# A 31-tap depthwise convolution divided anew between TensorE, VectorE, ScalarE and GpSimd

## The chip, the cores and the metric

The kernel runs on one core of a Trainium2 chip. The metric is the device time of one execution in microseconds, and what is told of a kernel is the median of several runs. All data is float32; a product of a weight matrix with activations is computed as three products of rounded halves ("hi" and "lo" parts), which a later section explains.

## What is computed

The reference is a stack of two transformer-like blocks, each with two layers, over 256 positions and 1024 channels. The change touches only the convolution branch of the second block's mixer. Cut to that:

```python
def depthwise_conv(c, w, b):                      # 31 taps, 512 channels
    pad = CONV_WIDTH_2 // 2                       # 15
    y = lax.conv_general_dilated(c, w.reshape(31, 1, 512), window_strides=(1,),
                                 padding=[(pad, pad)], feature_group_count=512, ...)
    return y + b

def second_block(x, ...):
    for i in range(2):
        h = x + 0.5 * swiglu(rms_norm_2(x, norm_ffn1[i]), w_ffn1_in[i], w_ffn1_out[i])
        u = rms_norm_2(h, norm_mix[i])
        q, k, v, c, g = jnp.split(u @ w_in[i], splits, axis=-1)
        y_attn = window_attention(q, k, v, sink[i], rel_bias) @ w_attn_out[i]
        c_val, c_gate = jnp.split(c, 2, axis=-1)
        c = c_val * jax.nn.sigmoid(c_gate)
        c = depthwise_conv(c, conv_w[i], conv_b[i])
        c = jax.nn.silu(layer_norm_2(c, conv_ln_g[i], conv_ln_b[i]))
        y_conv = c @ w_conv_out[i]
        g_attn, g_conv = jnp.split(jax.nn.sigmoid(g), 2, axis=-1)
        h = h + (g_attn * y_attn + g_conv * y_conv) @ w_o[i]
        ...
```

## The kernel before

Activations lie with channels on the 128 partitions and the 256 positions along the free axis (S = 256), so a convolution along positions is a sum over shifted columns, and one weight per partition. The 512 channels of the convolution are four chunks of 128, c0 to c3 (`conv(i, t)`, i = 0 to 3).

A weight matrix comes in pieces of 128 x 1024 (`wload`, L133). SP issues the transfer into `raw`; ScalarE casts it to `hi` (L145); VectorE makes `lo` = `raw` - `hi` (L146). Six buffers hold such splits, so a cast must wait until TensorE has done the products that read the buffer's old content. `mm3` (L182) then makes three products for each 128 rows: hi with h, hi with l, lo with h (L184, L185, L186), where h and l are the activations' halves (L221, a cast on ScalarE, and L222, a subtraction on VectorE).

`mix_b` is the mixer of the second block. It walks through 15 pairs of output columns of `w_in_2`, 48 products each: q, k and v (pairs 0 to 2), the four chunks of the convolution (3 to 6), and eight pairs of gates (`dp` 0 to 7). Beside them run generators: attention heads (`heads`, `attention_b`), and `conv` for each chunk. The class `Order` (L310) interleaves them: each `yield` names a cost, that cost times a pace of 1.5 sets when the generator is due again, and after each pair the planner moves on by 5.2 and lets all that is due write its instructions. A scheduler then sets the final order within each engine; every engine runs its own queue in order, and semaphores join them.

In `conv`, a chunk's gate is a tanh (L1203), and its product with the values goes into the padded tile `cp`, 286 columns, of which there are three buffers (L1208). The first PTAPS = 7 taps are matmuls: ScalarE makes a diagonal matrix `dg` from the identity and one column of weights (L1214, four buffers), and TensorE multiplies `cp`, shifted by the tap, with it and adds up in a PSUM tile `rec` (L1215). The pool of `rec` has two buffers. ScalarE then copies the sum with the bias into the SBUF tile `cy` (L1218), and VectorE adds the other 24 taps there one behind the other (L1220, `stt`: tap times weight plus `cy`).

When all chunks and heads have written their work, `norm` computes the layer norm over the 512 channels on TensorE: four matmuls with ones for the mean (L1243), four for the variance from squares (L1250, L1251), a square root on ScalarE with a table load of its own (L1254), the reciprocal on VectorE (L1256), then a tanh for silu (L1260) and the split into h and l (L221, L222). Its instructions are placed among the products of `w_mix` with the attention's result (four outputs, 24 products each); the products of `w_mix` with the convolution's result need the split. Elsewhere in the listing, L1104 are transposes of the softmax, L158 the attention's products (through `run`), L1085 to L1098 the softmax, L1107 the copies `pt` of the transposes, and L1233 the tanh of a gate.

Of the kernel before, what the change touches and what calls it, by code (L numbers as in the profile page):

```python
# [8 lines left out]
F32 = mybir.dt.float32  # L9
F32R = mybir.dt.float32r  # L10
AF = mybir.ActivationFunctionType
# [4 lines left out]
MUL, ADD, SUB, MAX = ALU.mult, ALU.add, ALU.subtract, ALU.max  # L16

S = 256
# [4 lines left out]
C1 = -0.5 * math.exp(-0.5)  # L23
ADA_EVERY = 0.67
ADA_BUFS = 2
PTAPS = 7
ADA_PE = 2
FILL = {("f", 0): ((0, 0), (0, 1)), ("f", 1): ((1, 0), (1, 1))}
PBANKS = (4, 2, 2)
# [1088 lines left out]
def mix_b(G, L, x, l, mp, bias, dbg=None):  # L1118
    nc = G.nc
    mm = nc.tensor.matmul  # L1120
    tt = nc.vector.tensor_tensor
    stt = nc.vector.scalar_tensor_tensor
    act = nc.scalar.activation
    ident = G.c("ident", 128)
# [5 lines left out]
    cwh = L.pool.tile([128, 124], F32, tag="cwh", name=G.nm("cwh"))  # L1130
# [68 lines left out]
    cy = [None] * 4  # L1199
    pmu = []  # L1200

    def conv(i, t):
        act(t[:, S:], t[:, S:], AF.Tanh, scale=0.5)  # L1203
        cp = mp.tile([128, S + 30], F32, tag="cp", name=G.nm("cp"), bufs=3)
        nc.vector.memset(cp[:, 0:15], 0.0)
        nc.vector.memset(cp[:, S + 15:], 0.0)
        yield 0.5
        stt(cp[:, 15:S + 15], t[:, S:], 1.0, t[:, :S], ADD, MUL)  # L1208
        dg = []
        yield 1.0  # L1210
        ps = G.rec()
        for jj in range(PTAPS):
            d = mp.tile([128, 128], F32, tag="dg", name=G.nm("dg"), bufs=4)
            act(d, ident, AF.Copy, scale=cwh[:, jj * 4 + i:jj * 4 + i + 1])  # L1214
            mm(ps[:, :S], d, cp[:, jj:jj + S], start=jj == 0, stop=jj == PTAPS - 1)  # L1215
        yield 0.5 * PTAPS
        y = mp.tile([128, S], F32, tag="cy", name=G.nm("cy"), bufs=4)
        act(y, ps[:, :S], AF.Identity, bias=L.col("cb", i))  # L1218
        for jj in range(PTAPS, 31):
            stt(y, cp[:, jj:jj + S], cwh[:, jj * 4 + i:jj * 4 + i + 1], y, MUL, ADD)  # L1220
            yield 0.6
        cy[i] = y

    for i in range(4):
        t = mp.tile([128, 512], F32, tag="cvg", name=G.nm("t"), bufs=1)
        tt(v3(t, 2), v3(pair(3 + i), 2), rb, MUL)
        O.add(f"c{i}", conv(i, t), 0.6)
        O.advance(cost)
# [55 lines left out]
    for dp in range(4):  # L1284
        w = G.wload(G.ins["w_o"][l, dp], 2048)
        for i in range(2):
            ps = G.ps()
# [320 lines left out]
```

## Time and profile before

| | us |
|---|---|
| median of 3 runs | 2260.83 |
| lowest and highest | 2255.63, 2268.85 |
| the profiled execution | 2264.67 |
| its span in the trace | 2262.9 |
| TensorE busy in it | 2204.6 (97%) |
| VectorE busy in it | 1681.6 (74%) |
| ScalarE busy in it | 1276.6 (56%) |

The profile page has for each engine the busy time, its share of the span and the number of instructions. PE is TensorE's matmul side, PEld its weight load, which runs beside it; DVE is VectorE, ACT ScalarE, POOL GpSimd. The two mixers lie at about 1290 to 1470 us and 1870 to 2050 us of the span; the convolution and the norm of the first at 1334 to 1439 us. A row of the timeline has the start, the time of the entry or group, the engine, the line, the operation and its operands; a bracket at the end tells how long the engine was idle before and what released it. Ends of matmuls are modelled, so a group's price is best read from starts. The clock granted to TensorE is nine tenths of full speed or more in every slice of the page, 0.991 over the span.

### The profile page before, as it was taken

Reading aid. Unit: us, or ns where it says so; the run is one execution under the profiler, and the core shown is the slowest. Engines: PE = TensorE matmul, PEld = TensorE weight load, DVE = VectorE, ACT = ScalarE, POOL = GpSimd, SP = SyncE. Lnnn points to the kernel's source line nnn. Section 1 sums busy time; section 2 is a strip of 40 time slices with the busy share of each in tenths; the row PEclk is TensorE's granted clock in tenths of the full one; section 3 lists DMA queues with packets and bytes.
Section 4 is the critical chain, followed back from the end, with each engine's and each line's share of the span. In section 5 each row is a group of like instructions: output and inputs, shape, how many; then the busy total and the mean of one; then the engine's idle time right before and its main releaser. Section 6 shows DMA issues by size and latency. Waiting matters only on the chain.

```text
span 2262.9 us, 46464 instructions
## 1 busy us (share of the span) xinstructions
PE 2204.6 (97%) x18878; PEld 2134.0 (94%) x18878; DVE 1681.6 (74%) x3041; ACT 1276.6 (56%) x2160; POOL 12.7 (1%) x26
## 2 busy tenths in 40 slices
PE   4999999999999999999999999999999999999999
PEld 4989999999888899999999999999999999999999
DVE  5787878877678878876576569976577656997665
ACT  3575645654567645655454567654465446765444
POOL 0000000000000000000100000000000000000000
PEclk9999999999999999999999999999999999999999
DMA  7644457867554356755775652655566565256553
GB/s 281 195 146 145 139 192 263 271 220 260 187 167 145 121 168 227 264 185 157 177 231 159 199 170 88 203 182 177 164 199 196 165 189 177 94 179 198 182 162 120
DMA packets 127522, 415.35 MB, mean 184 GB/s; under 512 B 15019, under 2 KB 17707, under 8 KB 127308
## 3 DMA queue, kind: packets, MB, share of 16 engines
q1 hardware_dynamic: 124668, 407.23, 57.2%
q0 software_dynamic: 768, 2.10, 0.6%
q8 instruction: 148, 2.42, 0.4%
q10 hardware_dynamic: 1872, 3.06, 0.4%
q14 instruction: 66, 0.54, 0.1%
HBM read 408.92 MB, written 3.41 MB: 182 GB/s over the span
## 4 chain that ended last, share of the span: by engine, by line
PE 61%; DVE 2%; ACT 1%; DMA 1%; issue 0%; SPq 0%; ACTq 0%; DVEq 0%
PE ps L184 19%; PE ps L185 19%; PE ps L186 19%; PE aux L158 1%; PE rec L1215 1%; DMA raw<-in_ffn_in 1%; DVE lo L146 1%; ACT hi L145 0%; PE aux L1104 0%; DMA raw<-in_w_out 0%; PE aux L268 0%; DMA raw<-in_ffn_up 0%; DVE cy L1220 0%; ACT dg L1214 0%; PE aux L282 0%
## 5 line engine op out<-in xcount | busy, mean ns | idle before, releaser
L184 PE MATMUL ps<-h,hi 128*128 128x256 f32 x5088 | 1439.1, 284 | 13.7 <-ACT h L221 8.8
L186 PE MATMUL ps<-h,lo 128*128 128x256 f32 x5088 | 1434.0, 282 | 1.2 <-DVE lo L146 1.2
L185 PE MATMUL ps<-l,hi 128*128 128x256 f32 x4032 | 1136.8, 283 | 4.1 <-DVE l L222 3.9
L145 ACT CAST hi<-raw 128x1024 fp32r<-128x1024 f32 (+1 forms) x724 | 704.4, 976 | 629.2 <-PE ps L185 406.4
L146 DVE TENSOR_TENSOR lo<-raw,hi 128x1024 fp32r<-128x1024 f32 (+1 forms) x724 | 819.5, 1134 | 318.8 <-ACT hi L145 316.5
L184 PEld LDWEIGHTS ps<-h,hi 128*128 128x128 f32 x5088 | 961.5, 189 | 25.2 <-ACT h L221 10.2
L186 PEld LDWEIGHTS ps<-h,lo 128*128 128x128 f32 x5088 | 962.0, 189 | 5.3 <-issue 2.2
L185 PEld LDWEIGHTS ps<-l,hi 128*128 128x128 f32 x4032 | 763.4, 189 | 10.2 <-DVE l L222 4.8
L185 PE MATMUL ps<-h,hi 128*128 128x256 f32 x1056 | 298.9, 283 | 0.0
L185 PEld LDWEIGHTS ps<-h,hi 128*128 128x128 f32 x1056 | 198.6, 188 | 1.9 <-issue 0.5
L221 ACT CAST h<-t 128x256 fp32r<-128x256 f32 x148 | 59.6, 405 | 135.4 <-DVE t L1034 93.6
L222 DVE TENSOR_TENSOR l<-t,h 128x256 fp32r<-128x256 f32 x148 | 62.6, 424 | 50.1 <-ACT h L221 50.0
L362 DVE SCALAR_TENSOR_TENSOR ada<-ada,cact 128x1024 f32<-128x1024 f32 x80 | 96.6, 1215 | 2.1 <-DMA ada<-in_w_ada 2.1
L1031 DVE TENSOR_TENSOR t<-ps,r 128x512 f32<-128x512 f32 x88 | 60.7, 690 | 39.3 <-PE ps L186 39.0
L1220 DVE SCALAR_TENSOR_TENSOR cy<-cp,cwh,cy 128x256 f32<-128x256 f32 x192 | 85.1, 477 | 3.2 <-ACT cy L1218 2.9
L235 ACT ACTIVATE t<-x 128x256 f32<-128x256 f32 x96 | 37.6, 406 | 16.8 <-DVE x L1002 7.7
L1034 DVE TENSOR_TENSOR t<-t,t 128x256 f32<-128x256 f32 x88 | 36.8, 419 | 7.2 <-ACT t L1033 7.2
L1033 ACT ACTIVATE t<-t 128x256 f32<-128x256 f32 x88 | 36.2, 412 | 8.5 <-DVE t L1031 7.6
L210 PE MATMUL ps<-hi,h 128*128 128x256 f32 x128 | 37.7, 294 | 0.0
L242 DVE TENSOR_TENSOR t<-t,t 128x256 f32<-128x256 f32 x87 | 36.5, 419 | 1.6 <-ACT t L237 0.3
L212 PE MATMUL ps<-lo,h 128*128 128x256 f32 x128 | 37.4, 293 | 0.0
L248 PE MATMUL aux<-ones,t 128*128 128x1 f32 x68 | 11.0, 267 | 20.9 <-DVE t L242 17.5
(325 smaller groups left out, 1959.8 us busy)
## 6 DMA issues: line engine op xcount, KB each, us to landing
raw<-in_w_in SPq DMA_DIRECT2D x176, 512.0 KB, 4.4
raw<-in_ffn_in SPq DMA_DIRECT2D x176, 512.0 KB, 4.5
raw<-in_ffn_up SPq DMA_DIRECT2D x88, 512.0 KB, 4.6
ada<-in_w_ada SPq DMA_DIRECT2D x80, 512.0 KB, 5.0
raw<-in_ffn_out SPq DMA_DIRECT2D x64, 384.0 KB, 3.1
raw<-in_ffn_out SPq DMA_DIRECT2D x64, 320.0 KB, 3.1
raw<-in_w_branch SPq DMA_DIRECT2D x24, 512.0 KB, 3.8
raw<-in_ffn_down SPq DMA_DIRECT2D x32, 384.0 KB, 3.5
```

What stands on the lines that cost most here:

```text
L145: nc.scalar.copy(hi[:, :m], raw[:, :m])
L146: nc.vector.tensor_tensor(lo[:, :m], raw[:, :m], hi[:, :m], SUB)
L184: mm(ps, w[0], x[0], start=first, stop=False)
L185: mm(ps, w[0], x[1], start=False, stop=False)
L186: mm(ps, w[1], x[0], start=False, stop=last)
L210: mm(ps[:, :256], x[k][0][:, sl], h, start=k == 0, stop=False)
L221: nc.scalar.copy(h, src)
L222: nc.vector.tensor_tensor(l, src, h, SUB)
L235: nc.scalar.square(sq, x[k])
L362: nc.vector.scalar_tensor_tensor(raw, raw, 1.0, cact, MUL, MUL, accum_out=mods[f // 8][:, f % 8:f % 8 + 1]))
L1031: nc.vector.tensor_tensor(v3(gu, 2), v3(ps, 2), rb, MUL)
L1220: stt(y, cp[:, jj:jj + S], cwh[:, jj * 4 + i:jj * 4 + i + 1], y, MUL, ADD)
```

## The change

Two constants replace PTAPS = 7: PTAPS = 5 and GTAPS = 8. For each chunk, five taps are diagonals and matmuls into `acc`, the first 256 columns of a `rec` tile. The next 18 taps are VectorE's; each reads and writes `acc` in that same PSUM bank. The last eight taps (jj = 23 to 30) are ScalarE's: the first writes tap times weight plus bias straight into `y`, the tile `cy`; the other seven write into a tile `cyt`, of which there is one buffer, and GpSimd adds that to `y`. In the end VectorE adds `acc` and `y` into `y`. Since `rec` has two buffers, chunks 2 and 3 wait in the plan until the chunk two before them is done. Line numbers move: the diagonals are L1226 in the new code, their matmuls L1227, VectorE's taps L1233, the closing addition L1235, the first scaled tap L1214, the others L1217, GpSimd's additions L1218, the gate's tanh L1247, the mean L1257, the squares L1264, the variance L1265, the square root L1268 and the norm's tanh L1274.

```diff
-PTAPS = 7
+PTAPS, GTAPS = 5, 8
...
         stt(cp[:, 15:S + 15], t[:, S:], 1.0, t[:, :S], ADD, MUL)
-        dg = []
+        def wt(jj):
+            return cwh[:, jj * 4 + i:jj * 4 + i + 1]
+
+        def other(jj):
+            if jj == 31 - GTAPS:
+                act(y, cp[:, jj:jj + S], AF.Identity, scale=wt(jj), bias=L.col("cb", i))
+            else:
+                u = mp.tile([128, S], F32, tag="cyt", name=G.nm("cyt"), bufs=1)
+                act(u, cp[:, jj:jj + S], AF.Copy, scale=wt(jj))
+                nc.gpsimd.tensor_tensor(y, y, u, ADD)
         yield 1.0
-        ps = G.rec()
+        while i >= 2 and cy[i - 2] is None:
+            yield 0.5
+        y = mp.tile([128, S], F32, tag="cy", name=G.nm("cy"), bufs=4)
+        acc = G.rec()[:, :S]
         for jj in range(PTAPS):
             d = mp.tile([128, 128], F32, tag="dg", name=G.nm("dg"), bufs=4)
-            act(d, ident, AF.Copy, scale=cwh[:, jj * 4 + i:jj * 4 + i + 1])
-            mm(ps[:, :S], d, cp[:, jj:jj + S], start=jj == 0, stop=jj == PTAPS - 1)
+            act(d, ident, AF.Copy, scale=wt(jj))
+            mm(acc, d, cp[:, jj:jj + S], start=jj == 0, stop=jj == PTAPS - 1)
         yield 0.5 * PTAPS
-        y = mp.tile([128, S], F32, tag="cy", name=G.nm("cy"), bufs=4)
-        act(y, ps[:, :S], AF.Identity, bias=L.col("cb", i))
-        for jj in range(PTAPS, 31):
-            stt(y, cp[:, jj:jj + S], cwh[:, jj * 4 + i:jj * 4 + i + 1], y, MUL, ADD)
+        rest = list(range(31 - GTAPS, 31))
+        for jj in range(PTAPS, 31 - GTAPS):
+            if rest and jj % 2:
+                other(rest.pop(0))
+            stt(acc, cp[:, jj:jj + S], wt(jj), acc, MUL, ADD)
             yield 0.6
+        tt(y, acc, y, ADD)
         cy[i] = y
```

The order of the work outside the two mixers is the same. Within them it moves on every engine; two places follow.

The first is ScalarE's queue in the first mixer, around the last diagonals of chunk c3. Before, `dg_17169` is the last of c3's seven diagonals, `rec_17150` their sum, and `pt` are copies of the attention's transposes:

```order
L1107 COPY pt_17587<-aux_17570 128x512
L1233 ACTIVATE gate_17506<-gate_17506 128x512
L1107 COPY pt_17598<-aux_17589 128x512
L1214 ACTIVATE dg_17163<-ca,cwh_16496 128x128
L1214 ACTIVATE dg_17166<-ca,cwh_16496 128x128
L1214 ACTIVATE dg_17169<-ca,cwh_16496 128x128
L1218 ACTIVATE cy_17266<-rec_17150,vec_5351 128x256
```

After, c3's diagonals are `dg_17675`, `17678`, `17681`, `17684` and `17687`; `cyt` from `cp_16955` is a scaled tap of c2, from `cp_17033` one of c3. The rows begin behind `dg_17684`:

```order
L1217 ACTIVATE cyt_17947<-cp_16955,cwh_16496 128x256
L1217 ACTIVATE cyt_17959<-cp_17033,cwh_16496 128x256
L1217 ACTIVATE cyt_17968<-cp_16955,cwh_16496 128x256
L1217 ACTIVATE cyt_17978<-cp_17033,cwh_16496 128x256
L1217 ACTIVATE cyt_17982<-cp_16955,cwh_16496 128x256
L145 CAST hi_18006<-raw_18004 128x1024
L1090 ACTIVATE sc_17649,st_17651<-sc_17649,st_17651 128x256 x2
L1091 ACTIVATE st_17651<-st_17651,sink_5353 128x2
L1090 ACTIVATE sc_17657,st_17659<-sc_17657,st_17659 128x256 x2
L1091 ACTIVATE st_17659<-st_17659,sink_5353 128x2
L1098 ACTIVATE sc_17649<-sc_17649,st_17651 128x256 x2
```

Here the diagonals of one chunk stood in a row; now the fifth, `dg_17687`, comes only behind these rows, a gate's tanh and a copy `pt`. Each row of L1217 waits for GpSimd's addition of the one before it.

The second place is TensorE's queue at the variance of the norm in the first mixer. `ps_17976` and `ps_18024` are the last two outputs of `w_mix` with the attention's result before, `ps_18064` the second of the four after; `rec_18011` and `rec_18051` are the variance. Before:

```order
L184 MATMUL ps_17976<-h_17960,hi_17966 128x256
L185 MATMUL ps_17976<-l_17961,hi_17966 128x256
L186 MATMUL ps_17976<-h_17960,lo_17967 128x256
L1251 MATMUL rec_18011<-t_18018,ones 128x256
L1251 MATMUL rec_18011<-t_18021,ones 128x256
L186 MATMUL ps_18024<-h_17715,lo_17973 128x256
L184 MATMUL ps_18024<-h_17830,hi_17972 128x256
```

After:

```order
L184 MATMUL ps_18064<-h_17954,hi_18012 128x256
L1265 MATMUL rec_18051<-t_18052,ones 128x256
L1265 MATMUL rec_18051<-t_18055,ones 128x256
L1265 MATMUL rec_18051<-t_18058,ones 128x256
L1265 MATMUL rec_18051<-t_18061,ones 128x256
L185 MATMUL ps_18064<-l_17955,hi_18012 128x256
L186 MATMUL ps_18064<-h_17954,lo_18013 128x256
```

Between the last variance matmul and the first product that needs the norm's result stood 70 products; now 53 stand there. On ScalarE one more weight cast (`hi_18359`) now stands between the square root and the norm's tanh.

## Rows read from the trace of the kernel before

**Rows 1.** The page: busy time of engines, and two of its costliest groups.

```profile
PE 2204.6 (97%) x18878; PEld 2134.0 (94%) x18878; DVE 1681.6 (74%) x3041; ACT 1276.6 (56%) x2160; POOL 12.7 (1%) x26
...
L146 DVE TENSOR_TENSOR lo<-raw,hi 128x1024 fp32r<-128x1024 f32 (+1 forms) x724 | 819.5, 1134 | 318.8 <-ACT hi L145 316.5
...
L1220 DVE SCALAR_TENSOR_TENSOR cy<-cp,cwh,cy 128x256 f32<-128x256 f32 x192 | 85.1, 477 | 3.2 <-ACT cy L1218 2.9
```

**Rows 2.** Busy time by window: PE, PEld, DVE, ACT, POOL; granted clock; DMA.

```profile
1334.00:1425.00 91.00, 90.86 (x683) 82.62 (x681) 86.88 (x197) 64.64 (x135) 0.00 (x0) 1.00 0.35 105
1908.00:1997.00 89.00, 88.75 (x672) 80.56 (x672) 84.80 (x196) 62.78 (x132) 0.00 (x0) 1.00 0.35 109
1440.00:1460.00 20.00, 20.00 (x170) 19.93 (x170) 17.78 (x31) 11.59 (x20) 0.00 (x0) 1.00 0.51 161
```

**Rows 3.** Waits of TensorE's load side, 1330 to 1445: us, times, longest.

```profile
PEld rec L1215 <- ACT dg L1214: 0.5, 1, 0.5
...
PEld ps L184 <- ACT h L221: 0.4, 1, 0.4
PEld rec L1215 <- DVE cy L1220: 0.3, 1, 0.3
```

**Rows 4.** Chain of waits, first mixer, TensorE's pieces: start, us, what.

```profile
1352.51 3.02 PE rec L1215 x14
...
1390.85 0.87 PE aux L1104 x8
1392.35 0.70 PE aux L158 x2
1393.05 3.22 PE rec L1215 x14
1396.27 1.06 PE aux L158 x6
...
1403.03 1.01 PE aux L158 x8
```

**Rows 5.** All work of GpSimd by line: the fills (busy us, mean ns).

```profile
L794 POOL MEMSET wz<- 128x512 f32 x4 | 2.1, 544 | 396.5 <-PE ps L186 343.3 <-PE aux L186 53.2
L379 POOL MEMSET lora<- 128x1024 f32 x2 | 1.9, 955 | 175.4 <-issue 175.1 <-POOLq L1599 0.3
```

**Rows 6.** Timeline of ScalarE, first mixer.

```profile
1335.46 0.98 ACT L1214 ACTIVATE dg<-ca,cwh 128x128 f32<-128x128 f32 x3
...
1402.02 0.51 ACT L1090 ACTIVATE sc<-sc,st 128x256 f32<-128x256 f32 x1 [0.28 <-DVE st L1088]
...
1403.21 1.03 ACT L145 CAST hi<-raw 128x1024 fp32r<-128x1024 f32 x1
1404.14 0.63 ACT L1233 ACTIVATE gate<-gate 128x512 f32<-128x512 f32 x1
1404.67 0.56 ACT L1107 COPY pt<-aux 128x512 f32<-128x512 f32 x1
1405.14 0.36 ACT L221 CAST h<-aux 128x256 fp32r<-128x256 f32 x1
1405.40 0.91 ACT L1098 ACTIVATE sc<-sc,st 128x256 f32<-128x256 f32 x2
```

**Rows 7.** Timeline of TensorE, first mixer: the variance.

```profile
1429.25 1.02 PE L1251 MATMUL rec<-t,ones 128*128 128x256 f32 x4
```

**Rows 8.** Chain of waits, first mixer: ends of the norm's path.

```profile
1430.39 1.28 ACT L1254
...
1438.17 0.41 ACT h L221
```

**Rows 9.** Durations of one line of VectorE with a PSUM source: ns least, median, most.

```profile
L996 DVE SCALAR_TENSOR_TENSOR t<-ps,vec,t x44: 472/477/480, 399.3 to 1045.5; 128x255 f32<-128x255 f32 x44
```

**Rows 10.** Timeline of VectorE: the first four taps of c0.

```profile
1339.74 2.05 DVE L1220 SCALAR_TENSOR_TENSOR cy<-cp,cwh,cy 128x256 f32<-128x256 f32 x4 [1.11 <-ACT cy L1218]
```

**Rows 11.** Waits of ScalarE, 1333 to 1380: us, times, longest.

```profile
ACT hi L145 <- PE ps L185: 14.3, 11, 1.9
```

## The prediction

> **What bounds the kernel now.** I read the page's busy line first: TensorE is busy 97% of the span, VectorE 74%, ScalarE 56%, GpSimd 1% [rows 1]. So time comes only from TensorE: from work that it no longer has, and from gaps. The change touches the two B mixers, so I then took the table of windows over the stretch in which each does its convolution, and beside it one stretch of products alone [rows 2]. There TensorE has no gap worth the name, 90.86 of 91.00 us in the first mixer and 88.75 of 89.00 in the second, and VectorE 86.88 and 84.80: it is nearly full as well, and its largest single piece is the conv's taps (477 ns each, 192 in the kernel [rows 1], 96 of them in each mixer). The stretch of products gives the price of one product: 20.00 us for 170, 0.118 us. Third, the list of waits of TensorE's loading side over the whole mixer shows what idle time there is to win: 0.5 us for a conv diagonal (L1215 on L1214), 0.3 for L1220, and 0.4 behind the norm for h of L221 [rows 3]. So no more than about 1.2 us of a mixer is waiting that the conv causes; the rest of any gain must be matmuls taken away.
>
> **Part A, the taps that leave TensorE.** Two taps of each of four chunks, 8 taps per mixer. The chain has seven taps as 14 entries (each fp32 matmul is two) in 3.02 us, and another seven in 3.22 [rows 4]: 0.43 and 0.46 per tap. TensorE is on the path there, so they count in full: 8 x 0.43 = 3.45 us per mixer, 6.9 in all (at 0.46, 7.4). I take -6.9, range -6.5 to -7.4.
>
> **Part B, the wait for c1's diagonal.** It cost 0.5 us in this mixer [rows 3]. After, five diagonals are wanted instead of seven; c1's fifth is queued on ScalarE behind one weight cast (0.93, from its start to the next start), a scaled tap and itself, 1.8 us; five taps of TensorE take 5 x 0.43 = 2.15. So it should be there: -0.5 per mixer, -1.0 in all (0 to -1.6, if the 0.3 on L1220 goes too).
>
> **Part C, a new wait: c3's last diagonal behind five scaled taps.** This is where the order moved against the kernel. ScalarE makes a scaled tap, GpSimd adds it, and since `cyt` has one buffer, the next scaled tap waits for that addition. GpSimd's price isn't in the trace as an addition; what is there are fills, 544 ns for 512 columns and 955 for 1024 [rows 5]: 0.80 ns a column and 0.13 fixed. A fill of 256 columns would be 0.34. An addition has three streams (two in, one out) against the fill's one: from 0.34 (if they run abreast) to 3 x 0.34 = 1.02; I take three streams with the fixed part once, P = 0.13 + 3 x 0.205 = 0.75 us. A scaled tap is as L1098 of the same form, two in 0.91 us, 0.5 one alone [rows 6].
>
> Let T0 be the end of gate pair 4's products. On ScalarE follow, by the starts in [rows 6]: a cast 0.93, a gate 0.53, a diagonal (three in 0.98) 0.33, a copy pt 0.47, three diagonals, and a pt that waits for transposes which end at T0 + 3.6; with it and c3's fourth diagonal T0 + 4.4. Then five scaled taps with four additions waited for, 5 x 0.5 + 4 x 0.75 = 5.5; then a cast 0.93, two softmax sets of 1.19, two L1098 0.91, gate 0.53, pt 0.47 and at last the fifth diagonal 0.33: T0 + 15.4. On TensorE stand before c3's fifth matmul, by [rows 4]: eight transpose entries 0.87; c2's five taps 5 x 0.46 = 2.3; transposes 0.44 (half of 0.87); attention products 0.70; four products 0.47; attention 1.06; 44 products 44 x 0.118 = 5.19; transposes 0.44; attention 1.01; four taps 1.84: T0 + 14.3. So TensorE waits 1.1 us: +2.2 in all. Nothing useful stands behind the waiting matmul that could go first, since TensorE's queue is in order. At P = 0.34 there is no wait; at P = 1.5 it is 4.1 per mixer. Bounds here: 0 to +8.2.
>
> **Part D, the tail behind the norm.** The second half of the mixing products needs h of the normalised chunks. Before, the path from the last two variance matmuls (four entries from 1429.25, 1.02 long [rows 7]) through the square-root table, VectorE and ScalarE to the end of h at 1438.58 (1438.17 + 0.41 [rows 8]) takes 8.3 us; in that time TensorE does the 70 products that stand between them, 70 x 0.118 = 8.2, and 0.4 of waiting for h is listed [rows 3]. After, the four variance matmuls stand later and 53 products are left: 6.2 us. The path itself is as long as before (the one cast added ahead of the tanh table can lie beside the 1.28 us table load [rows 8] and VectorE's reciprocal). So +2.0 per mixer, +4.0 in all (0 if the variances become ready earlier, since then the path starts at the same distance; +6 if the added cast, which waits for the ring, pushes the tanh back by its 0.93).
>
> **Part E, VectorE.** 24 taps of a chunk become 18, and one closing addition comes: 5 instructions x 4 chunks x 2 = 40 fewer, 5 x 0.45 = 2.2 us a chunk less. VectorE isn't the bound, so this is cover, not gain. Taps now read and write a PSUM bank. A tap that reads PSUM isn't dearer: L996 has one PSUM source and takes 477 ns, as L1220 does [rows 1, 9]; a PSUM destination isn't shown, and I take 0.41 to 0.48, as tap behind tap; the dependent chain of four in 2.05 us, 0.51 each [rows 10], is the upper end. Is the last chunk still in time? After c3's fifth matmul VectorE has 24 taps (10.6 at 0.44), two closing additions (0.8), five L146 (5 x 1.134 = 5.7 [rows 1]) and some 4 of softmax and gates: 21.3; TensorE has about 23 us of other work before c3's mean matmul. Margin some 2 us: 0 (at 0.51 a tap +0.6 per mixer at most).
>
> **Part F, ScalarE while c0 and c1 run.** Ten diagonals and 24 scaled taps, 10 x 0.33 + 24 x 0.42 = 13.4 us, take the place of 21 diagonals and three evacuations, 8.2: 5.2 more. Six scaled taps stand back to back and wait for GpSimd, 6 x 0.75 = 4.5. This stretch had 14.3 us in which ScalarE's casts merely waited for TensorE to free the ring [rows 11], and that hides it; of it 4.7 go, because TensorE reaches T0 sooner by eleven taps of 0.43 (two each of c0 and c1, and c2's seven, which now come later). So 9.7 us of load stand against 9.6 of cover. Followed cast by cast, the latest comes 0.75 us late, where I estimate 2.1 us of slack before TensorE wants it. Cost 0, with 1.4 us to spare; without that cover each further us would land on TensorE through the casts (L145, then L146). GpSimd itself has nothing else in the mixers, and SP's queue is the same row for row.
>
> **The sum.** -6.9 - 1.0 + 2.2 + 4.0 = -1.7 us: of the gain three quarters are given back. The profiled run is at 2264.67, so 2263.0 there; it lies 3.8 above the median 2260.83 (2255.63 to 2268.85), so against the median 2259.1. About 0.5%, 11.3 us, is what a measurement of this kernel can tell from no change.
>
> **What a page of the notes says.** The fills give P = 0.75 only by a guess about streams. The Trainium skill, "GPSIMD Engine Reference", section 3.1, sets an fp32 addition on GpSimd at 1.96 times VectorE's time for the same one. No run here shows it; by it and VectorE's 0.42 for this shape P would be 0.82, an estimate from that page, and the sum -1.1.
>
> **Rivals.** (R1, slower) GpSimd's round trip is long, because an addition is slow in itself or because it must stand behind a VectorE instruction. Place: the four waits in part C and the six in part F. Price per mixer: 4 (P - 0.75) + max(0, 6 (P - 0.75) - 1.4). It decides (over +11.3) from P = 1.55 us. If an addition has to wait for one L146 (1.134 us [rows 1]) on top of its own 0.75, P is about 1.9 to 2: 5 + 6.1 per mixer, 22 in all, 2281. For it: VectorE is 95% busy there (86.88 of 91.00 us [rows 2]), so an addition that needed anything of it would seldom find it idle. Against: no row shows an engine held up by another's running instruction. The Trainium skill, "SBUF — State Buffer", section "Who interferes with whom", makes this a rule: a GpSimd operation that reads SBUF and a VectorE operation with two SBUF inputs exclude each other for a whole instruction, while a VectorE operation with at most one SBUF input doesn't contend. Nothing in this trace bears on it, since GpSimd has only 26 instructions here, none in the conv. By it only the additions that meet an L146 or another instruction with two SBUF inputs would pay, and not those that meet a tap in PSUM. I give R1 0.16.
>
> (R2, faster) The waits of C and D don't come, for instance because GpSimd is at 0.34 and the variances come earlier. Then A and B stand alone: -7.9, up to -9.0 with the upper ends: 2252 to 2253. It isn't over 0.5% unless more goes, such as casts that come sooner: chance that it comes so far 0.09; that it lies between, 0.2, inside "within 0.5%".
>
> (R3, VectorE) PSUM as destination makes each tap 0.51 or more. VectorE then has 72 taps x 0.05 = 3.6 us more per mixer, mostly inside what it saved; only the end of c3 shows: +1 to +2 in all, 2261. Chance 0.1, the same class. If a tap in PSUM were 0.6 or more, VectorE would become the bound and the norm would start later; I hold that for 0.03; with R1 it makes 0.19 on the slow side.
>
> **How the numbers follow.** Likeliest is the sum, 2259 (chance 0.42 with its bounds; with R2's inner part and R3 0.72 within 0.5%). Slower by over 0.5% (above 2272) 0.19, faster by over 0.5% (below 2249.5) 0.09. For eight in ten I go from 2250 (A and B at their upper ends, and a little) to 2278 (R1 with P just under 2).
>
> **What would show it.** A: the first conv matmul of a chunk to its last, 10 entries instead of 14, at 0.43 a tap, and 32 fewer TensorE entries (18846). B: no wait of L1227 for L1226 in c1. C: among TensorE's waits one of L1227 on L1226 near 1.1 us in each mixer, and on ScalarE gaps on GpSimd in front of L1217 of about P. D: a wait of L184 on L221 behind the norm of some 2.4 us instead of 0.4. E: L1233 at 0.41 to 0.5 us. F: no longer waits of L184 to L186 on L145 or L146 than before in the stretch of c0 and c1. The forecast is wrong if an addition on GpSimd with its wait is over 1.5 us, if VectorE's taps are 0.6 us in PSUM, or if the waits of D fail to come.

## The result

| | before | after |
|---|---|---|
| median of 6 runs, us | 2261.23 | 2275.94 |
| lowest and highest, us | 2255.63, 2268.85 | 2271.95, 2280.87 |
| ratio, 95% interval | | 1.0053, 1.0039 to 1.0068 |
| the profiled execution, us | 2264.67 | 2271.95 |
| its span, us | 2262.9 | 2270.2 |

The change made the kernel slower: by 0.53%, 12 us, by the ratio, while the two medians lie 14.7 us apart. The time lies in the range given (2250 to 2278), but the forecast was 2259, a gain of 1.7 us, and the interval leaves out both no change and any gain.

The profiled executions are 7.3 us apart, half of that. To see where it lies I counted TensorE's entries in both traces: outside the mixers they are the same, entry for entry. A stretch of 1250 entries that begins 150 entries ahead of the first conv tap, and ends at the same product behind the mixer (32/2 = 16 entries earlier in the count after), took 161.06 us before and 168.54 after in the first mixer, 161.02 and 166.70 in the second: +7.5 and +5.7. Behind and between them all stretches agree within 0.05 us. The part ahead of them, in which nothing was changed, happened to be 5.7 us shorter in this execution. So the change costs about 13 us, between the 12 of the ratio and the 14.7 of the medians, and the sum of the prediction (-0.9 per mixer) has to be held against +7.5 and +5.7. "Mixers" below are these two differences against the kernel before.

The page after, for [rows 1]; columns as there:

```profile
PE 2200.4 (97%) x18846; PEld 2129.4 (94%) x18846; DVE 1675.2 (74%) x3001; ACT 1294.7 (57%) x2200; POOL 59.7 (3%) x82
...
L1218 POOL TENSOR_TENSOR cy<-cy,cyt 128x256 f32<-128x256 f32 x56 | 47.0, 838 | 814.5 <-DVE hv L1156 501.5
L1233 DVE SCALAR_TENSOR_TENSOR rec<-cp,cwh,rec 128x256 f32<-128x256 f32 x144 | 65.5, 481 | 0.8
...
L1217 ACT ACTIVATE cyt<-cp,cwh 128x256 f32<-128x256 f32 x56 | 28.4, 507 | 21.7 <-POOL cy L1218 21.7
```

VectorE's taps in the PSUM bank are as long as those in SBUF were (481 against 477 ns), an addition of GpSimd has a mean of 838 ns, and ScalarE stood for 21.7 us behind additions, at 28 of the 56 scaled taps. Waits of TensorE's load side in the first mixer, 1320 to 1455, for [rows 3]:

```profile
PEld rec L1227 <- ACT dg L1226: 3.0, 3, 1.7
PEld aux L290 <- issue: 2.7, 1, 2.7
PEld ps L184 <- ACT h L221: 2.2, 1, 2.2
...
PEld aux L158 <- DVE sc L1085: 0.8, 1, 0.8
PEld ps L185 <- DVE l L222: 0.8, 1, 0.8
```

The first row has the wait forecast in part C (1.7 of the 3.0 us; the others are c1's and c2's), the third that of part D. The second, on L290, stood in no part. It is the transposition back of a head norm's factors, and the timelines show how it came to be late: ScalarE's and VectorE's rows, then TensorE's.

```profile
1347.22 0.51 ACT L1217 ACTIVATE cyt<-cp,cwh 128x256 f32<-128x256 f32 x1 [1.47 <-POOL cy L1218]
1348.58 0.51 ACT L1217 ACTIVATE cyt<-cp,cwh 128x256 f32<-128x256 f32 x1 [0.85 <-POOL cy L1218]
1349.00 1.03 ACT L145 CAST hi<-raw 128x1024 fp32r<-128x1024 f32 x1
...
1350.78 1.28 ACT L1150 ACT_TABLE_LOAD   x1
1352.07 0.21 ACT L1150 ACTIVATE hv<-hv 128x8 f32<-128x8 f32 x1
```

```profile
1347.56 0.16 DVE L1149 TENSOR_SCALAR hv<-hv 128x8 f32<-128x8 f32 x1
1350.06 1.22 DVE L146 TENSOR_TENSOR lo<-raw,hi 128x1024 fp32r<-128x1024 f32 x1 [2.34 <-ACT hi L145]
...
1355.25 1.12 DVE L1158 TENSOR_TENSOR t<-hv,hv 128x512 f32<-128x512 f32 x1
```

```profile
1356.51 1.42 PE L290 MATMUL aux<-ca,t 128*128 128x128 f32 x8 [2.52 <-DVE t L1158]
```

VectorE has the variance ready (L1149) at 1347.7. ScalarE takes its square root (L1150) at 1352.07, since it works off its queue and stands twice behind an addition; VectorE idles 2.34 us for a cast that is late for the same reason; the rest of the norm reaches TensorE 2.52 us late. ScalarE's waits over that stretch, 1325 to 1358, are these alone:

```profile
ACT cyt L1217 <- POOL cy L1218: 5.8, 8, 1.5
```

Its waits for TensorE to free a weight buffer, the cover of [rows 11], are gone here; in the same part of the kernel before, 1331 to 1364, they were 9.9 us. And the idle time had a second price. Windows (columns as in [rows 2]) behind it, in the first mixer:

```profile
1357.00:1362.00 5.00, 5.00 (x32) 5.00 (x32) 4.09 (x7) 2.45 (x4) 0.00 (x0) 0.66 0.43 139
1362.00:1371.00 9.00, 9.00 (x77) 8.49 (x76) 7.06 (x19) 6.84 (x10) 1.47 (x2) 1.00 0.38 119
```

The granted clock is 0.66 there, a mean over 1.2 and 2.4 GHz: 14 products start 0.21 us apart instead of 0.118, 1.3 us. Behind the same idle time of the second mixer, which ends at 1935.4, it stayed at 1.00, and that is a good part of the difference between +7.5 and +5.7:

```profile
1930.00:1942.00 12.00, 9.50 (x82) 9.33 (x81) 11.45 (x29) 9.33 (x13) 2.24 (x3) 1.00 0.40 119
```

Where "Mixers" of two runs are compared below, a stretch of some 3 us at 1.2 GHz in one of them can account for 0.9 to 1.5 us.

### The profile page after: what moved, and what is told of

Read it like the earlier page. It is cut to its first block, busy times and chain, and to the rows that moved or that the text cites. A ratio compares the mean times of both kernels' runs of the same rounds, so it can differ in the third digit from the quotient of the medians.

```text
span 2270.2 us, 46468 instructions
## 1 busy us (share of the span) xinstructions
PE 2200.4 (97%) x18846; PEld 2129.4 (94%) x18846; DVE 1675.2 (74%) x3001; ACT 1294.7 (57%) x2200; POOL 59.7 (3%) x82
## 4 chain that ended last, share of the span: by engine, by line
PE 57%; DVE 3%; ACT 3%; DMA 1%; issue 1%; POOL 1%; SPq 0%; DVEq 0%; ACTq 0%
PE ps L185 18%; PE ps L184 18%; PE ps L186 18%; ACT hi L145 1%; DVE lo L146 1%; POOL cy L1218 1%; DMA raw<-in_ffn_in 1%; PE aux L158 0%; ACT cyt L1217 0%; DVE rec L1233 0%; ACT dg L1226 0%; DMA raw<-in_w_out 0%; PE aux L268 0%; DMA raw<-in_ffn_up 0%; ACT L1203 0%
## 5 line engine op out<-in xcount | busy, mean ns | idle before, releaser
L146 DVE TENSOR_TENSOR lo<-raw,hi 128x1024 fp32r<-128x1024 f32 (+1 forms) x724 | 821.9, 1137 | 325.2 <-ACT hi L145 323.3
L222 DVE TENSOR_TENSOR l<-t,h 128x256 fp32r<-128x256 f32 x148 | 62.6, 423 | 49.6 <-ACT h L221 49.5
L1218 POOL TENSOR_TENSOR cy<-cy,cyt 128x256 f32<-128x256 f32 x56 | 47.0, 838 | 814.5 <-DVE hv L1156 501.5
L1233 DVE SCALAR_TENSOR_TENSOR rec<-cp,cwh,rec 128x256 f32<-128x256 f32 x144 | 65.5, 481 | 0.8
L1217 ACT ACTIVATE cyt<-cp,cwh 128x256 f32<-128x256 f32 x56 | 28.4, 507 | 21.7 <-POOL cy L1218 21.7
```

The source lines that it names most:

```text
L146: nc.vector.tensor_tensor(lo[:, :m], raw[:, :m], hi[:, :m], SUB)
L222: nc.vector.tensor_tensor(l, src, h, SUB)
L1218: nc.gpsimd.tensor_tensor(y, y, u, ADD)
L1233: stt(acc, cp[:, jj:jj + S], wt(jj), acc, MUL, ADD)
```

## The experiments

Times are medians with the ratio to the kernel before, run on the same chip. Mixers are as defined above. The second and the seventh run leave work out and only show what it costs.

| run | TensorE, VectorE, ScalarE taps | us | ratio (95%) | mixers, us |
|---|---|---|---|---|
| after | 5, 18, 8 | 2275.94 | 1.0053 (1.0039 to 1.0068) | +7.5, +5.7 |
| e1_more_buffers | 5, 18, 8 | 2267.31 | 1.0020 (1.0008 to 1.0031) | +1.9, +0.8 |
| e2_no_additions | 5, 18, 8 | 2264.61 | 1.0002 (0.9991 to 1.0014) | -0.3, +0.6 |
| e3_early_diagonals | 5, 18, 8 | 2283.40 | 1.0089 (1.0072 to 1.0106) | +10.8, +9.5 |
| e4_no_scaled_taps | 5, 25, 1 | 2295.95 | 1.0139 (1.0121 to 1.0157) | +14.5, +15.0 |
| e5_seven_taps | 7, 16, 8 | 2264.72 | 1.0008 (0.9995 to 1.0020) | +0.1, +0.2 |
| e6_psum_only | 7, 23, 1 | 2301.79 | 1.0168 (1.0146 to 1.0190) | +18.9, +19.0 |
| e7_shorter_last_chunk | 5, 18 (12 in c3), 8 | 2258.68 | 0.9984 (0.9973 to 0.9996) | -2.6, -2.7 |
| e8_third_bank | 5, 25, 1 | 2293.67 | 1.0151 (1.0126 to 1.0176) | +17.0, +18.0 |
| e9_before_with_wait | 7, 24, 0 | 2297.15 | 1.0146 (1.0128 to 1.0164) | +15.4, +16.2 |
| e10_buffers_and_bank | 5, 18, 8 | 2264.53 | 1.0014 (0.9999 to 1.0028) | +1.1, +1.3 |
| e11_ten_scaled_taps | 5, 16, 10 | 2260.22 | 0.9985 (0.9974 to 0.9996) | -2.2, -1.0 |
| e12_four_taps | 4, 16, 11 | 2256.95 | 0.9956 (0.9938 to 0.9973) | -3.6, -3.4 |

### One buffer for the scaled tap

```diff
-                u = mp.tile([128, S], F32, tag="cyt", name=G.nm("cyt"), bufs=1)
+                u = G.tmp(S)
```

> The changed kernel, but the scaled tap goes into the ring of eight small temporaries instead of the one buffer cyt, so ScalarE need not wait for each GpSimd addition. Theory 1 (the round trip over one buffer holds ScalarE's whole queue, and through it weight casts, the square root of the head norm and c3's last diagonal): in each mixer the 2.5 us wait before L290 and the half clock behind it (1.4 us in the first mixer), the 0.7 us wait on L1085 and c3's 1.45 us go, about 5 us per mixer; 2264 to 2267. The wait of 2.3 us behind the norm stays. Theory 2 (GpSimd's additions delay VectorE's L146 themselves, 1.59 instead of 1.22 us, and that is what costs): the additions are still there, so 2273 to 2277, and the 2.5 us wait stays. Theory 3 (the order in which c0 and c1 now stand costs, not the wait): no change either, 2274 to 2278.

```diff
-                nc.gpsimd.tensor_tensor(y, y, u, ADD)
+                pass
```

> The changed kernel with GpSimd's 56 additions left out (seven taps of each chunk are made and not added), still one buffer cyt. Theory 1: ScalarE waits for nothing, same gain as with more buffers, 2264 to 2267. Theory 2: here, and only here, L146 is back at 1.22 us at most; if that is the cost, 2264 to 2267 here against 2273 to 2277 with more buffers. Theory 3: 2274 to 2278 in both.

With eight buffers the mixers lose 5.6 and 4.9 us of their delay, as theory 1 had it, though the time, 2267.31, is just above its range. ScalarE never waits for GpSimd, and the wait on L290 is gone from the list of the same stretch. There is no less work ahead of that square root than in the changed kernel: the scheduler has now placed 19 scaled taps there instead of 17, beside the same 14 diagonals. So it is the waiting, not the amount of work, that made it late. Of the forecast waits that behind the norm stands, and the one behind L1085, which theory 1 counted among its own, stands too:

```profile
PEld ps L184 <- ACT h L221: 2.3, 1, 2.3
...
PEld ps L185 <- DVE l L222: 0.9, 2, 0.8
PEld aux L158 <- DVE sc L1085: 0.8, 1, 0.8
...
PEld rec L1227 <- ACT dg L1226: 0.7, 1, 0.7
```

Leaving the additions out instead, with the one buffer kept, makes the first mixer 2.2 us shorter than eight buffers do, the second 0.2, and the median 2.7. In the second mixer the granted clock was 0.50 for some 3 us without additions, and stayed at 1.00 with eight buffers; without such stretches the additions are worth 1.7 to 1.8 us in either mixer (an estimate: products at 0.21 instead of 0.118 us taken off in both runs). So theory 2 holds as a small part; the wait behind L1085 belongs to it, as it falls from 0.8 to 0.4. How the two engines meet is seen in the changed kernel, GpSimd's rows first, then VectorE's:

```profile
1333.33 0.74 POOL L1218 TENSOR_TENSOR cy<-cy,cyt 128x256 f32<-128x256 f32 x1 [3.47 <-ACT cyt L1217]
1334.70 1.73 POOL L1218 TENSOR_TENSOR cy<-cy,cyt 128x256 f32<-128x256 f32 x1 [0.62 <-ACT cyt L1217]
...
1340.06 0.74 POOL L1218 TENSOR_TENSOR cy<-cy,cyt 128x256 f32<-128x256 f32 x1 [0.62 <-ACT cyt L1217]
```

```profile
1332.63 2.06 DVE L1233 SCALAR_TENSOR_TENSOR rec<-cp,cwh,rec 128x256 f32<-128x256 f32 x4
1334.60 1.22 DVE L146 TENSOR_TENSOR lo<-raw,hi 128x1024 fp32r<-128x1024 f32 x1
...
1340.29 1.59 DVE L146 TENSOR_TENSOR lo<-raw,hi 128x1024 fp32r<-128x1024 f32 x1
```

The addition at 1333.33 runs beside taps in the PSUM bank and takes 0.74. The one at 1334.70, begun 0.1 us after an L146, takes 1.0 us more. The L146 at 1340.29, begun while an addition ran, takes 1.59 instead of 1.22. Without additions none is longer than 1.23, of 30 in 1320 to 1440 (least, median, most in ns):

```profile
L146 DVE TENSOR_TENSOR lo<-raw,hi x30: 1175/1222/1228, 1319.1 to 1437.4; 128x1024 fp32r<-128x1024 f32 x30
```

That is what the Trainium skill, "SBUF — State Buffer", "Who interferes with whom", says of a GpSimd read and a VectorE operation with two SBUF inputs: the one that begins first holds the other up, and taps whose second operand is in PSUM don't take part. The trace agrees, with 0.74 against 1.73 us and 1.22 against 1.59.

### Diagonals

```diff
-            d = mp.tile([128, 128], F32, tag="dg", name=G.nm("dg"), bufs=4)
+            d = G.tmp(S)[:, :128]
```

> The changed kernel, but diagonals take the ring of eight temporaries instead of four buffers dg, so that the fifth of a chunk needs no buffer that TensorE must free first; cyt keeps its one buffer. Theory 1: only the waits for the fifth diagonals go (1.5 us for c3, 0.5 us for c1 and 0.3 for c2), some 2 us per mixer, 2271 to 2273; the 2.5 us before L290 stays. A rival (those diagonals are late because ScalarE is late in general): no change, 2274 to 2278.

Both theories missed the time. The diagonals did come early enough, but the time rose to 2283.40. In ScalarE's queue 18 diagonals instead of 14 now stand ahead of that head norm's square root, and the wait on L290 is 5.8 us instead of 2.7:

```profile
PEld aux L290 <- issue: 5.8, 1, 5.8
```

It says the same as the first run from the other side: ScalarE was full there, its waits for additions included, and what is put ahead pushes the square root. Four diagonals are 1.2 us; the rest of the 3.1 us more was not traced. With eight buffers for the scaled taps, 18 diagonals stand ahead as well in the fifth run below, and there is no wait on L290.

### What the scaled taps pay for

```diff
-PTAPS, GTAPS = 5, 8
+PTAPS, GTAPS = 5, 1
```

> The changed kernel with GTAPS = 1: five taps on TensorE, 25 on VectorE in the PSUM bank, one on ScalarE, GpSimd none. Theory 1: all waits on GpSimd go, TensorE keeps its eight taps less per mixer (-7 us in all), and 28 taps of VectorE come back per mixer (28 x 0.45 = 12.6 us), which stretches it where it is 95% busy: 2256 to 2266, c3's end and the mean matmuls late by up to 3 us per mixer. If instead the accumulation in PSUM or the move to five taps itself costs: 2270 or more.

```diff
-PTAPS, GTAPS = 5, 8
+PTAPS, GTAPS = 7, 1
```

> The changed kernel with PTAPS = 7 and GTAPS = 1: seven taps on TensorE as before, 23 on VectorE in the PSUM bank, one on ScalarE, nothing on GpSimd. Against the kernel before only the place of VectorE's sum has changed, and that c2 and c3 wait in the plan for a bank. Theory 1 with VectorE as the bound and PSUM no dearer: 24 VectorE instructions per chunk as before, 2258 to 2265. Rival (holding a bank for all of VectorE's taps is what delays c2 and c3): c3's mean matmul waits 5 us or more in each mixer, 2275 to 2295.

The fourth run missed by 30 us: without the scaled taps it is among the four slowest. In the first mixer TensorE waits 8.8 us for the closing addition of c3, and 5.3 for the norm. Much the same holds for the sixth, which has VectorE's load of the kernel before; it is 7 us above even its rival's range. TensorE's waits, 1320 to 1465, of the fourth and then the sixth:

```profile
PE rec L1257 <- DVE cy L1235: 8.8, 1, 8.8
PE ps L184 <- ACT h L221: 5.3, 1, 5.3
```

```profile
PE rec L1257 <- DVE cy L1235: 7.7, 1, 7.7
PE ps L184 <- ACT h L221: 5.3, 1, 5.3
```

That could be the PSUM bank as a place, the bank as something held, or the wait for it in the plan. Two runs tell them apart.

```diff
 # the kernel before
+        while i >= 2 and cy[i - 2] is None:
+            yield 0.5
         ps = G.rec()
         for jj in range(PTAPS):
```

> The kernel before (seven taps on TensorE, 24 on VectorE in SBUF) with one thing added: c2 and c3 wait in the plan until the chunk two before them is written out, as in the changed kernel. Theory 1 (that wait, and not the place of VectorE's sum, is what delays the convolution's end where VectorE has 24 or more taps): c2's first tap moves from 36 us after the mixer's start mark to 85 or more, the mixer gets 15 to 20 us longer, 2290 to 2303. Rival (the sum in the PSUM bank is slower): 2260 to 2266.

```diff
 # as e4_no_scaled_taps
-PBANKS = (4, 2, 2)
+PBANKS = (3, 2, 3)
...
-        while i >= 2 and cy[i - 2] is None:
+        while i >= 3 and cy[i - 3] is None:
```

> As the run without scaled taps (GTAPS = 1, 25 taps on VectorE), but with three buffers for the accumulating bank and three instead of four for the products, and c2 needs no wait for c0. Theory 1 (VectorE's work is what makes the mean wait 9.1 us there): the wait stays within 2 us, 2290 to 2298. Rival (the wait for a bank delays c2 and c3): the wait falls below 3 us, 2262 to 2275.

The wait alone, in the kernel before with its sums in SBUF, costs 15.4 and 16.2 us per mixer. Some 12 us of each is idle time of TensorE (5.8 for c3, 1.0 and 5.3 in the norm); the granted clock was 0.50 from 1444 to 1460, and what ran there at 1.2 GHz has a share in the rest. So the place in PSUM is not what makes the sixth run slow; the 3.5 and 2.8 us that it takes beyond this one are not explained. How the wait comes to cost that is seen in the taps of c0, c1, c2 and c3 on TensorE (timeline; for the kernel before c2 and c3 are in [rows 4], at 1352.51 and 1393.05, with c0 at 1334.43):

```profile
1338.44 3.18 PE L1217 MATMUL rec<-cp,dg 128*128 128x256 f32 x14
1347.55 3.31 PE L1217 MATMUL rec<-cp,dg 128*128 128x256 f32 x14
1411.12 3.29 PE L1217 MATMUL rec<-cp,dg 128*128 128x256 f32 x14
1420.34 3.19 PE L1217 MATMUL rec<-cp,dg 128*128 128x256 f32 x14
```

From c0 to c2 it is 72.7 us instead of 18, to c3 81.9 instead of 58.6. VectorE runs out of taps meanwhile. Over 86.56 us from c0's first tap it is busy for 75.11 us; over as long from the same point it was 82.55 before, 7.4 more (fourth number after the window, first the run with the wait, then the kernel before):

```profile
1338.44:1425.00 86.56, 86.56 (x656) 79.58 (x656) 75.11 (x162) 63.23 (x132) 0.00 (x0) 1.00 0.43 133
```

```profile
1334.43:1421.00 86.57, 86.43 (x653) 79.26 (x652) 82.55 (x191) 62.63 (x131) 0.00 (x0) 1.00 0.33 100
```

The missing work then stands at the end, where TensorE has nothing else. A third bank doesn't help where VectorE has 25 taps: c2 then begins early, shares VectorE with c0 and c1, and c0, for which c3 waits, is done all the later: its closing addition ends 71.6 us after its first tap, in the fourth run 58.1. In the changed kernel this wait is there too (c2 at 57.3 us after c0). That it costs far less there goes with the eight taps of ScalarE and GpSimd: the fourth run, without seven of them, has its first mixer at +14.5, the first run at +1.9. They do not add to the gain of TensorE's two taps; they make up for what the wait would cost.

### What sets the end

```diff
 # as e1_more_buffers
-PTAPS, GTAPS = 5, 8
+PTAPS, GTAPS = 7, 8
```

> As the first run (scaled taps in the ring of eight temporaries), but seven taps on TensorE again and 16 on VectorE. Theory 1 (the chain of VectorE's taps for c3, the norm and its tail sets the end of the mixer; two taps less on TensorE only leave it waiting there): the eight taps cost TensorE 3.45 us per mixer, and the 2.4 and 0.8 us of waiting behind the norm go, so the time stays near the first run's, 2264 to 2269. Rival (the wait behind the norm has to do with the order of the variance and the added cast, not with how long VectorE takes): the wait stays, and the time is the first run's plus 6.9, 2273 to 2276.

```diff
 # as e1_more_buffers
-            stt(acc, cp[:, jj:jj + S], wt(jj), acc, MUL, ADD)
+            if i < 3 or jj < 17:
+                stt(acc, cp[:, jj:jj + S], wt(jj), acc, MUL, ADD)
```

> As the first run, but six of VectorE's 18 taps of the last chunk c3 are left out. Theory 1 (VectorE's taps of c3 set when the norm comes): c3 ends 2.5 to 3 us sooner, the waits of 2.4 and 0.8 us behind the norm fall to 0.5 or less, 2260 to 2263. Rival (the tail itself, from the variance on, is what is longer than its cover): they stay, 2266 to 2269.

```diff
 # as e1_more_buffers
-PBANKS = (4, 2, 2)
+PBANKS = (3, 2, 3)
...
-        while i >= 2 and cy[i - 2] is None:
+        while i >= 3 and cy[i - 3] is None:
```

> As the first run, with three buffers for the accumulating bank and three instead of four for the products; only c3 waits, for c0. Theory 1 (with 18 taps VectorE's own work, shared by whichever chunks are under way, sets the end, so that an earlier c2 only makes c0 and c1 later): c2's taps at 34 instead of 70 us, but the last closing addition still at 107 to 110 us, and 2264 to 2270. Rival (the bank's wait delays the end): the last closing addition 4 us or more earlier, the waits behind the norm gone, 2258 to 2262.

With seven taps again and 16 on VectorE, TensorE has 6.9 us more to do than in the first run and the time is 2 to 3 us shorter (the intervals overlap, so what is sure is that it isn't 6.9 longer): two taps of TensorE are worth nothing while VectorE ends late. The wait behind the norm is back to 0.5:

```profile
PEld ps L184 <- ACT h L221: 0.5, 1, 0.5
```

Six taps of VectorE less in c3, with five on TensorE, take the mixers 4.5 and 3.4 us below the first run, and the time, 2258.68, is below the range of either theory; the gap behind the norm is then 0.6. So it is the end of VectorE's taps, not the tail behind the variance, that lengthens it. c3's closing addition came 7 to 8 us sooner, not the 2.5 to 3 expected, and why so much is not shown. The third bank brings c2 forward (16 us after c0) and leaves the last closing addition where it was, 91 us after c0's first tap in both; the wait behind the norm is 2.1 us there too, and the time is the first run's within the interval. Why c3 ends so late even then, with 18 taps on VectorE instead of 24, stays open.

### Two versions that follow

```diff
 # as e1_more_buffers
-PTAPS, GTAPS = 5, 8
+PTAPS, GTAPS = 5, 10
...
-            if rest and jj % 2:
+            if rest and jj % 3:
```

> As the first run, with GTAPS = 10 instead of 8 (16 taps of VectorE, ten of ScalarE with nine additions of GpSimd), handed out at two of three steps. Theory 1: VectorE ends c3 about 4 us sooner, as with six of c3's taps left out; the waits of 2.4 and 0.8 us behind the norm go, and what five taps save on TensorE stays: mixers 2 to 3 us shorter than before, 2255 to 2259. Rival (ScalarE, with eight scaled taps more per mixer, gets late with casts): waits on L145 or L146 come up, 2262 to 2270.

```diff
 # as e11_ten_scaled_taps
-PTAPS, GTAPS = 5, 10
+PTAPS, GTAPS = 4, 11
```

> As the run with ten scaled taps, but four taps on TensorE, 16 on VectorE and eleven on ScalarE (ten additions of GpSimd). Theory 1: VectorE has as much as there, so the conv ends as soon, TensorE loses four taps more per mixer (1.7 us), and ScalarE has the room for four scaled taps instead of four diagonals: mixers 1.5 us shorter than in that run, about 3 us in all, 2255 to 2259 beside 2262 for the kernel before. Rival (ScalarE or GpSimd is late by then, or VectorE again sets the end): no gain over that run or a loss, 2259 to 2266.

Both beat the kernel before: by 0.15%, just clear of no change and 1.2 us above the range of theory 1, and by 0.44% (0.27 to 0.62%), within it. Of the latter's waits in the first mixer none is over 0.9 us, and that behind the norm is no longer among them; the first of the list:

```profile
PEld ps L184 <- issue: 1.8, 5, 0.4
PEld aux L1104 <- ACT pt L1107: 1.2, 2, 0.9
```

## Why the prediction was wrong, part by part

**A, TensorE's taps: right in size.** Ten entries of c0's taps take 2.32 us with their modelled end, 0.46 a tap, or 0.43 from start to start, and 32 entries went. But as the fifth run shows, the gain was not free to take while VectorE had 18 taps.

**B: wrong in sign.** c1's fifth diagonal did not come in time; TensorE stands idle 0.40 us for it, and c1 loses 0.3 us more than in the kernel before:

```profile
1336.69 1.89 PE L1227 MATMUL rec<-cp,dg 128*128 128x256 f32 x8
1338.98 0.70 PE L1227 MATMUL rec<-cp,dg 128*128 128x256 f32 x2 [0.40 <-ACT dg L1226]
```

I had let one cast and one scaled tap stand ahead of it and counted no wait of that tap for GpSimd; there it stood behind an addition (1338.13, released by GpSimd).

**C: right.** c3's fifth diagonal was forecast 1.1 us late; its entries start 1.67 us apart where 0.22 is normal, 1.45 us, in both mixers. The five scaled taps stand on ScalarE as forecast, with four waits of 0.84 to 0.85 us for additions. P was 0.74 in the undisturbed case, forecast 0.75. The ratio of 1.96 that the Trainium skill, "GPSIMD Engine Reference", section 3.1, states would have given 0.82, an estimate; the trace has 0.74 against VectorE's 0.42, a ratio of 1.76. With eight buffers the wait of c3's diagonal goes, as it must if this account is right; c2's is the 0.7 us that stays in that list.

**D: right in size, short in reason.** Forecast +2.0 per mixer; the gap ahead of the first product of the normalised chunks is 2.30 and 2.29 against 0.43, +1.9, and 0.5 to 0.9 more for L222. I had put it down to the 53 products behind the variance. The number is right, but those are the sign and not the cause: the variance stands later because c3 ends later on VectorE. In the first mixer its last tap ends 89.0 us behind c0's first in the kernel before, with 486 products started, and 97.2 us behind it after, with 504; in the seventh run, where it ends sooner, the gap is 0.6.

**E: right for a tap, blind to the wait.** L1233 takes 481 ns. (The sum of 21.3 us comes to 21.1.) I took the wait of c2 and c3 in the plan for a mere detail of order and gave it no price. In the kernel before it costs 15 to 16 us per mixer. How much of it is left in the changed kernel is not shown: the third bank removed c2's part of it, and D's wait stayed.

**F: the step that failed.** I set 9.7 us of load on ScalarE against 9.6 of cover and put the lateness at 0.75 us with 2.1 of slack, at a cost of 0. Three things were wrong. The waits for GpSimd were eight and 5.8 us instead of six and 4.5 (additions beside an L146 took up to 1.73). I followed the casts alone, while the head norm's square root stood in the same queue and had less slack than they. And TensorE was granted half the clock behind 2.5 us of idle time in the first mixer. Together: not 0 but 2.5 us for L290 in each mixer, and 1.3 for the clock in the first; eight buffers took both away. The load as a whole was not far off: over 1327 to 1374, the stretch of [rows 11], 3.8 us of cover were left. It was gone where the square root stood.

Two terms more stood in no part: some 0.7 for L158 behind L1085, which eight buffers leave and which halves without additions, and 0.8 for the clock behind the norm (9 products at 0.21).

In the first mixer: -3.5 (A), +0.3 (B), +0.3 (c2's fifth diagonal, 0.49 instead of 0.22), +1.5 (C), +2.6 (D with L222), +2.5 (F), +0.7 (L1085), +2.1 (clock, 1.3 of it F's) = 6.5 of the 7.5 measured; the last 1.0 I didn't trace. R1's price formula was for additions of 1.55 us and more; at a mean of 0.838 it gives +0.35 per mixer. So R1 as I had put it did not come either. Its place, ScalarE's queue behind GpSimd, was the right one, and its threshold wrong: my 1.4 us of room in part F did not exist there. That the time lies in the range is luck, since the range's upper end came from R1 with P just under 2.

## What to carry to other kernels

A helper engine that is fed through a single buffer can make the feeding engine wait for each item (here for 28 of 56), and that engine's queue holds much else: list everything that stands behind the wait, the short steps of a long chain above all, and not only the kind of work that is counted in the sum. Spare time of an engine over a stretch is no slack for a given instruction. When a resource is held longer than before (here a bank for all of VectorE's taps), price first the wait that this forces on the next user, by putting that wait alone into the old kernel.

## What the runs showed of the hardware

An addition of 128 x 256 in fp32 on GpSimd took 0.74 us undisturbed (fills of that size were estimated at 0.34), and 1.05 to 1.73 when it began while an L146 ran, a VectorE subtraction with both inputs in SBUF; the subtraction took 1.37 to 1.63 instead of 1.22 when it began while an addition ran. VectorE adding up in a PSUM bank was neither slower (481 against 477 ns) nor in GpSimd's way. After the same 2.5 us of idle TensorE, the clock was granted at 1.2 GHz for some 3 us in one mixer and not in the other. In the mixers of the kernel after, the first three runs and the tenth, TensorE stood idle for 2.0 to 2.5 us twelve times, and the granted clock fell to 1.2 GHz with nine of them.
